# A hybrid decoder step: the split weights begin at eight byte offsets

## The chip, the cores and the metric

The kernel runs on one core of one Trainium2 chip. The metric is the device time of one execution in microseconds (us). The kernel before took 1399.37 us, the median of three runs (1398.88 to 1400.08).

## What is computed

One inference step of one decoder layer for 256 prompt tokens and 8 sample tokens, 264 columns in all, with a model width of 2048, in float32. What matters here is that it is mostly products of activations with large weight matrices:

```python
def _layer(x, mem_k, mem_v, k_buf, v_buf, ssd_conv_past, ssd_h0, ffn_past, w):
    proj = rms_norm(x, w['g_mix']) @ w['w_in']                 # 2048 x 6688
    q, k, v, z, xbc, dt_raw = jnp.split(proj, IN_SPLITS, axis=-1)
    ...
    x = x + jnp.concatenate([attn, ssd], axis=-1) @ w['w_out']  # 3072 x 2048
    x = x + cross_attend(x, mem_k, mem_v, w['g_cross'], w['w_cq'], w['cq_norm_g'], w['w_co'])
    f, new_ffn = conv_ffn(x, ffn_past, w['g_ffn'], w['w_up'], w['ffn_conv_w'], w['ffn_conv_b'],
                          w['w_down'])                          # 2048 x 11264, 5632 x 2048
    return x + f, (new_k, new_v, new_conv, new_h, new_ffn)
```

Between the products lie a sliding-window attention, a Mamba-2 scan, a cross-attention into 256 memory tokens and two short convolutions.

## The kernel before, in words

Activations are kept with features on the partitions and the 264 tokens along the free dimension: a tile of eight blocks holds 8 x 264 float32 values in each partition, so one block begins 1056 bytes behind the last. Each float32 operand of a large product is split into a high part, rounded to the type float32r, and a low part, which is the difference. Three products of the parts, each a float32r matmul, stand for one float32 product: high x high, high x low, low x high. That is `mm3` (lines 99 to 102): for each 128 x 128 block of weights, line 100 multiplies the high weights with the high activations, line 101 the high weights with the low activations, line 102 the low weights with the high activations. The weights are the stationary operand, so every matmul has its own weight load; only in `v_pair`, for the matrix w_cv, the memory tokens are stationary and the weights move.

`weights` (line 72) brings a weight unit of 2048 float32 values per partition in two parts of 1024 (NPART). For each part it issues one DMA from SyncE's queue into a buffer `wraw` (line 79), casts it to the high tile `whi` on ScalarE (line 85) and subtracts on VectorE to the low tile `wlo` (line 86). Each of the three tags has four buffers of 4096 bytes per partition (WBUFS is 4, line 67), used in turn; a buffer is written again when TensorE has done with the part that lay in it. The pool of these tiles is allocated ahead of the pools of the activations, and the sizes are multiples of 32 bytes.

`proj` (line 104) loops over units, over the parts of a unit, over two output blocks m and over the four k of a part, and calls `mm3`: a part is 2 x 4 x 3 = 24 matmuls, and the slice of weights that one matmul loads begins at k x 1024 + m x 512 bytes within the part. The first part of a unit goes with the activation blocks k 0 to 3 of a tile of eight, the second with k 4 to 7. For an output accumulated in a PSUM bank, `evac` takes it out on VectorE.

The opening of the kernel works on eight parts that arrive in blocks together with the activations; `w_piece` (line 171) allocates their high and low tiles from the same buffers and cuts them into two k of 512 columns. Everything after it goes through `weights`. An `up` block of the feed-forward stage multiplies two units of w_up with the activations X2 (x2h, x2l), a `down` block one unit of w_down with hh and hl.

Three other places are touched by the prediction: line 1359 writes the tile u from its element 2 (`u[:, 2:]`), line 1404 adds a result to the aligned slices of the residual, and lines 686 and 708 are the sample attention's matmuls with the cached keys kcT (rows of 129 elements) and values vc (rows of 128).

The order of most work is left to a planner that keeps the program's order per engine, with priorities for the weights; the opening is in an order written out by hand.

Of the kernel before, what the change touches and what calls it, by code (L numbers as in the profile page):

```python
# [8 lines left out]
F32R = mybir.dt.float32r  # L9
# [38 lines left out]
def hybrid_decoder_step_kernel(ctx: ExitStack, tc: tile.TileContext, I, O):  # L48
# [4 lines left out]
    wpool = ctx.enter_context(tc.tile_pool(name="wpool", bufs=2))  # L53
# [6 lines left out]
    def psum(tag):  # L60
        return ps.tile([128, 512], F32, tag=tag, name=tag, bufs=banks[tag])
# [4 lines left out]

    NPART, WBUFS = 1024, 4

    def raw_part(n=NPART):
        return wpool.tile([128, n], F32, tag="wraw", name="wraw", bufs=4)  # L70

    def weights(src, n=2048, into=None):

        out = []
        with tc.high_priority():
            for o in range(0, n, NPART):
                w = min(NPART, n - o)
                x = raw_part(w)
                nc.sync.dma_start(out=x, in_=src[:, o:o + w])
                if into:  # L80
                    hi, lo = into
                else:
                    hi = wpool.tile([128, w], F32R, tag="whi", name="whi", bufs=WBUFS)
                    lo = wpool.tile([128, w], F32R, tag="wlo", name="wlo", bufs=WBUFS)
                S.copy(out=hi, in_=x)  # L85
                V.tensor_tensor(out=lo, in0=x, in1=hi.bitcast(F32), op=ALU.subtract)  # L86
                out.append((hi, lo))
        return out
# [15 lines left out]
    def proj(units, acts, evac, n=T, nb=2, tag="mm"):  # L104

        outs = [psum(t) for t in (tag if isinstance(tag, list) else [tag] * nb)]
        for ui, (src, act) in enumerate(zip(units, acts)):
            parts = src if isinstance(src, list) else weights(src)
            for pi, (wh, wl) in enumerate(parts):
                wh = wh.rearrange("p (k c) -> p k c", c=128 * nb)  # L110
                wl = wl.rearrange("p (k c) -> p k c", c=128 * nb)
                nk = wh.shape[1]
                for m in range(nb):
                    for k in range(nk):
                        kk = pi * nk + k
                        ah, al = act(8 * ui + kk) if callable(act) else (act[0][:, kk, :n], act[1][:, kk, :n])
                        last = mm3(outs[m][:, :n], wh[:, k, m * 128:(m + 1) * 128], wl[:, k, m * 128:(m + 1) * 128],
                            ah, al,
                            ui == 0 and kk == 0, ui == len(units) - 1 and kk == nk * len(parts) - 1)
                if ui == 0:  # L120
                    marks["part"] = last
        for m in range(nb):
            with tc.high_priority():
                evac(m, outs[m][:, :n])
# [44 lines left out]
    pre = {}  # L169

    def w_piece(k, n):
        if k % 2 == 0:
            pre[k // 2] = [wpool.tile([128, NPART], F32R, tag=t, name=t, bufs=WBUFS).rearrange("p (k c) -> p k c", c=512)
                           for t in ("whi", "wlo")]
        return blocks[k // 4][:, k % 4:k % 4 + n, T:], *(w[:, k % 2:k % 2 + n, :] for w in pre[k // 2])

    def w_split(k, n, half=False):
        raw, hi, lo = w_piece(k, n)
        if half:
            V.tensor_copy(out=hi[:, :, 0:256], in_=raw[:, :, 0:256])  # L180
            S.copy(out=hi[:, :, 256:512], in_=raw[:, :, 256:512])
        else:
            S.copy(out=hi, in_=raw)
        return lambda: V.tensor_tensor(out=lo, in0=raw, in1=hi.bitcast(F32), op=ALU.subtract)
# [9 lines left out]
    with tc.manual_schedule(engines={mybir.EngineType.SP, mybir.EngineType.PE, mybir.EngineType.Activation, mybir.EngineType.DVE}):  # L194
# [21 lines left out]
        for k in range(6):  # L216
            x_hi(k)
            lo = w_split(k, 1, k < 2)
            x_lo(k)
            lo()  # L220
        for k in range(6, KB, 2):
            x_hi(k)
            x_hi(k + 1)
            lo = w_split(k, 2)
# [200 lines left out]
    p = psum("y")  # L425
# [40 lines left out]
    p = psum("x")  # L466
# [5 lines left out]
    p = psum("x")  # L472
# [301 lines left out]
    for c in range(2):  # L774
        p = psum("x")
# [4 lines left out]
    for w, XT in enumerate((BT, CT)):  # L780
        p = psum("x")
# [71 lines left out]
    p = psum("x")  # L853
# [349 lines left out]
    def v_pair(i):  # L1203
        pv = [psum("mm") for _ in range(2)]
        for u in range(2):
            parts = [w.rearrange("p (k c) -> p k c", c=256) for hl in weights(I["w_cv"][2 * i + u]) for w in hl]
            nk = parts[0].shape[1]
            for k in range(8):
                wh, wl = parts[2 * (k // nk)], parts[2 * (k // nk) + 1]
                mhi, mlo = mem_hl(8 * u + k)  # L1210
                for c in range(2):
                    cs = slice(c * 128, c * 128 + 128)
                    mm3(pv[c][:, 0:256], mhi[:, cs], mlo[:, cs], wh[:, k % nk, :], wl[:, k % nk, :],
                        u + k == 0, u == 1 and k == 7)
        for c in range(2):
            S.activation(out=vx[:, c, 256 * i:256 * i + 256], in_=pv[c][:, 0:256], func=AF.Copy, scale=rmc[:, 0, c:c + 1])
# [15 lines left out]
    p = psum("y")  # L1232
# [45 lines left out]
    for pi, (wh, wl) in enumerate(weights(I["w_co"][0])):  # L1278
        wh, wl = (w.rearrange("p (k c) -> p k c", c=512) for w in (wh, wl))
        for k in range(2):  # L1280
            h = 2 * pi + k
            for m in range(4):
                ms = slice(m * 128, m * 128 + 128)
                mm3(outs[m][:, :T], wh[:, k, ms], wl[:, k, ms], OH[:, h, :], OL[:, h, :], h == 0, h == 3)
# [4 lines left out]
    for u in range(1, 4):  # L1289
        with tc.issue_after(heads[0].ins), tc.issue_after(heads[1].ins):  # L1290
            proj([I["w_co"][u]], [(OH, OL)], lambda m, pm, u=u: x2_ev(4 * u + m, pm), nb=4,
                 tag=[cyc[(4 * (u - 1) + m) % 5] for m in range(4)])
# [264 lines left out]
def build(shapes):  # L1557

    import concourse.bacc as bacc

    nc = bacc.Bacc("TRN2", target_bir_lowering=False, num_devices=1)
    ins = {n: nc.dram_tensor(f"in_{n}_dram", s, dt, kind="ExternalInput").ap() for n, (s, dt) in shapes.items()}
    outs = {n: nc.dram_tensor(f"out_{n}_dram", s, F32, kind="ExternalOutput").ap() for n, s in _OUTS}
    with tile.TileContext(nc, schedule_with_timeline_sim=True) as tc:
        hybrid_decoder_step_kernel(tc, ins, outs)
    return nc
# [10 lines left out]
```

## Time and profile before

| | |
|---|---|
| median of three runs | 1399.37 us (1398.88 to 1400.08) |
| span of the profiled execution, first to last instruction | 1397.1 us |
| the median less that span | 2.3 us |
| TensorE matmul, busy | 1392.5 us, 11535 matmuls |
| weight loads (PEld), busy | 1367.8 us, 11535 loads |
| VectorE, busy | 1052.1 us (75%) |
| ScalarE, busy | 769.3 us (55%) |
| GpSimd, busy | 95.4 us (7%) |
| moved by DMA | 298.33 MB, mean 214 GB/s |

In the rows of the profile, PE is TensorE's matmul, PEld its weight load, DVE VectorE, ACT ScalarE, POOL GpSimd and SP SyncE. L85 is line 85 of the kernel. A row of a group names the output and input tiles (without buffer numbers), the shapes, the count, the busy time in us and the mean ns of one, and the idle time of the engine just before them with what ended most of it. Matmuls overlap, and their ends are modelled, so the busy time of PE is no measure of how well it is used; the starts of the instructions are.

### The profile page before, as it was taken

To read this page: it belongs to the slowest core of one execution; us is meant where nothing else is said; L and a number is where in the kernel's file an instruction comes from. 1 tells how busy PE (TensorE), PEld (TensorE's weight loads), DVE (VectorE), ACT (ScalarE), POOL (GpSimd) and SP (SyncE) were. 2 spreads that over 40 slices of the span, in tenths; PEclk is the share of its full clock that TensorE was granted. 3 is DMA by queue.
4 is the path that set the end of the run, shared out by engine and by line. 5 is a ranking of instruction groups with operands and counts; after the bars stand their busy time and mean duration, and the time that the engine had idled before them with its cause. 6 is when DMAs were issued, how large, how long until landed. Compare 5 with 4: busy or idle time off the path is not lost.

```text
span 1397.1 us, 29012 instructions
## 1 busy us (share of the span) xinstructions
PE 1392.5 (100%) x11535; PEld 1367.8 (98%) x11535; DVE 1052.1 (75%) x1874; ACT 769.3 (55%) x1255; POOL 95.4 (7%) x286
## 2 busy tenths in 40 slices
PE   9999999999999999999999999999999999999999
PEld 9999999999999999899999999999999999999998
DVE  7879799999987774578777775777577757765654
ACT  7667756556545554566565544554455445543532
POOL 0000011121000000002010000000000000000000
PEclk9999999999999999999999999999999999999999
DMA  7954467777777567565576765676567656655664
GB/s 299 323 162 135 139 217 245 233 239 253 235 221 240 182 237 263 209 251 191 186 255 213 255 208 187 211 254 211 185 211 239 197 184 197 196 180 183 191 185 138
DMA packets 89479, 298.33 MB, mean 214 GB/s; under 512 B 12032, under 2 KB 17152, under 8 KB 88832
## 3 DMA queue, kind: packets, MB, share of 16 engines
q1 hardware_dynamic: 83840, 277.61, 60.5%
q0 software_dynamic: 5504, 18.88, 4.1%
q8 instruction: 90, 1.47, 0.4%
q14 instruction: 45, 0.37, 0.1%
HBM read 280.77 MB, written 16.23 MB: 213 GB/s over the span
## 4 chain that ended last, share of the span: by engine, by line
PE 100%; DVE 0%; issue 0%
PE mm L100 21%; PE mm L101 21%; PE mm L102 21%; PE t L100 10%; PE t L102 10%; PE t L101 10%; PE t L240 1%; PE y L825 1%; PE t L278 1%; PE y L841 0%; PE s L240 0%; PE mm L240 0%; PE x L278 0%; PE t L559 0%; PE x L1137 0%; PE s L1184 0%
## 5 line engine op out<-in xcount | busy, mean ns | idle before, releaser
L85 ACT CAST whi<-wraw 128x1024 fp32r<-128x1024 f32 x440 | 459.9, 1048 | 530.6 <-PE mm L101 278.3
L86 DVE TENSOR_TENSOR wlo<-wraw,whi 128x1024 fp32r<-128x1024 f32 x440 | 541.8, 1233 | 221.1 <-ACT whi L85 217.3
L100 PE MATMUL mm<-x2h,whi 128*128 128x264 f32 x704 | 199.8, 284 | 0.0
L100 PE MATMUL t<-x2h,whi 128*128 128x264 f32 x704 | 199.8, 284 | 0.0
L102 PE MATMUL t<-x2h,wlo 128*128 128x264 f32 x704 | 199.7, 284 | 0.0
L101 PE MATMUL mm<-x2l,whi 128*128 128x264 f32 x704 | 199.6, 284 | 0.0
L101 PE MATMUL t<-x2l,whi 128*128 128x264 f32 x704 | 199.5, 283 | 0.0
L102 PE MATMUL mm<-x2h,wlo 128*128 128x264 f32 x704 | 199.3, 283 | 0.0
L101 PE MATMUL mm<-hl,whi 128*128 128x264 f32 x704 | 198.7, 283 | 0.0
L102 PE MATMUL mm<-hh,wlo 128*128 128x264 f32 x704 | 198.2, 283 | 0.0
L100 PE MATMUL mm<-hh,whi 128*128 128x264 f32 x704 | 197.2, 284 | 0.0
L100 PE MATMUL mm<-xh,whi 128*128 128x264 f32 x576 | 164.7, 287 | 0.0
L101 PE MATMUL mm<-xl,whi 128*128 128x264 f32 x576 | 164.5, 287 | 0.0
L102 PE MATMUL mm<-xh,wlo 128*128 128x264 f32 x576 | 162.8, 287 | 0.0
L101 PEld LDWEIGHTS mm<-x2l,whi 128*128 128x128 f32 x704 | 132.6, 188 | 0.0
L100 PEld LDWEIGHTS t<-x2h,whi 128*128 128x128 f32 x704 | 132.5, 188 | 0.0
L101 PEld LDWEIGHTS t<-x2l,whi 128*128 128x128 f32 x704 | 132.5, 188 | 0.0
L101 PEld LDWEIGHTS mm<-hl,whi 128*128 128x128 f32 x704 | 132.4, 188 | 0.0
L100 PEld LDWEIGHTS mm<-x2h,whi 128*128 128x128 f32 x704 | 132.4, 188 | 0.0
L102 PEld LDWEIGHTS t<-x2h,wlo 128*128 128x128 f32 x704 | 132.2, 188 | 0.0
L102 PEld LDWEIGHTS mm<-x2h,wlo 128*128 128x128 f32 x704 | 132.1, 188 | 0.0
L102 PEld LDWEIGHTS mm<-hh,wlo 128*128 128x128 f32 x704 | 132.0, 188 | 0.0
(506 smaller groups left out, 2950.7 us busy)
## 6 DMA issues: line engine op xcount, KB each, us to landing
wraw<-in_w_up_dram SPq DMA_DIRECT2D x176, 512.0 KB, 4.4
wraw<-in_w_in_dram SPq DMA_DIRECT2D x96, 512.0 KB, 4.7
wraw<-in_w_dn_dram SPq DMA_DIRECT2D x88, 512.0 KB, 4.3
wraw<-in_w_out_dram SPq DMA_DIRECT2D x48, 512.0 KB, 4.4
h<-in_h_dram POOLq DMA_DIRECT2D x32, 256.0 KB, 4.6
hn<-in_h_dram SPq DMA_DIRECT2D x16, 512.0 KB, 4.8
out_state_s_dram<-hn POOLq DMA_DIRECT2D x16, 512.0 KB, 3.5
e<-dram_la SPq DMA_DIRECT2D x16, 256.0 KB, 5.5
```

Source lines behind the costliest of these rows:

```text
L85: S.copy(out=hi, in_=x)
L86: V.tensor_tensor(out=lo, in0=x, in1=hi.bitcast(F32), op=ALU.subtract)
L100: PE.matmul(out, wh, xh, start=start, stop=False)
L101: PE.matmul(out, wh, xl, start=False, stop=False)
L102: return PE.matmul(out, wl, xh, start=False, stop=stop)
L240: PE.matmul(first[c][:, :T], pre[k // 2][i][:, k % 2, c * 128:(c + 1) * 128], A[k // 8][x][:, k % 8, :], start=k + i + x == 0, stop=k == K ...
L278: return PE.transpose(out, in_, cst[0:k, C_ID:C_ID + k])
L825: PE.matmul(y[o:o + 64, (h // 2) * 128:(h // 2) * 128 + 128], xdt[:, h, :], es[h // 4][:, h % 4, :], start=True, stop=True)
```

## The change

The buffers of `whi` and `wlo` become 24 float32 elements (96 bytes) longer, and a part no longer begins at the start of its buffer: the high part begins at the element that a list of eight gives for the part's number modulo 8, the low part at another entry, which shifts by one every eight parts. In bytes the entries are 0, 16, 32, 48, 64, 80, 8 and 4. The eight parts of the opening keep offset 0 in the longer buffers. The four buffers of a tag lie 4192 bytes apart instead of 4096, and the tiles allocated behind them move by 768 bytes. `wraw`, the number and kind of the instructions and their order are left as they are.

```diff
     NPART, WBUFS = 1024, 4
 
+    WSLACK, WSTART = 24, (0, 4, 8, 12, 16, 20, 2, 1)
+    part_no = [0]
+
+    def offsets():
+        n = part_no[0]
+        part_no[0] += 1
+        return WSTART[n % 8], WSTART[(n + n // 8) % 8]
+
...
-                    hi = wpool.tile([128, w], F32R, tag="whi", name="whi", bufs=WBUFS)
-                    lo = wpool.tile([128, w], F32R, tag="wlo", name="wlo", bufs=WBUFS)
+                    hi, lo = (wpool.tile([128, NPART + WSLACK], F32R, tag=t, name=t, bufs=WBUFS)[:, a:a + w]
+                              for t, a in zip(("whi", "wlo"), offsets()))
...
-            pre[k // 2] = [wpool.tile([128, NPART], F32R, tag=t, name=t, bufs=WBUFS).rearrange("p (k c) -> p k c", c=512)
+            pre[k // 2] = [wpool.tile([128, NPART + WSLACK], F32R, tag=t, name=t, bufs=WBUFS)[:, 0:NPART].rearrange("p (k c) -> p k c", c=512)
```

## The prediction

> **What bounds the kernel now.** I read the page from the top: busy times, the chain of work that ended last, then the groups.
>
> ```profile
> span 1397.1 us, 29012 instructions
> PE 1392.5 (100%) x11535; PEld 1367.8 (98%) x11535; DVE 1052.1 (75%) x1874; ACT 769.3 (55%) x1255; POOL 95.4 (7%) x286
> ...
> PE 100%; DVE 0%; issue 0%
> ...
> L85 ACT CAST whi<-wraw 128x1024 fp32r<-128x1024 f32 x440 | 459.9, 1048 | 530.6 <-PE mm L101 278.3
> L86 DVE TENSOR_TENSOR wlo<-wraw,whi 128x1024 fp32r<-128x1024 f32 x440 | 541.8, 1233 | 221.1 <-ACT whi L85 217.3
> L100 PE MATMUL mm<-x2h,whi 128*128 128x264 f32 x704 | 199.8, 284 | 0.0
> ```
>
> TensorE is on the chain for all of the span, so whatever happens to one matmul or one weight load is paid 10,000 times over, and whatever happens to ScalarE or VectorE is not paid until it makes TensorE late. The two instructions that write the tiles of this change have that room: the 440 casts on ScalarE have 530.6 us of idle time just before them, 278.3 of it spent on TensorE to let go of a buffer; the 440 subtractions on VectorE have 221.1 us, nearly all of it spent on the cast. They are made ahead of need and held up by TensorE, not the reverse.
>
> The 284 ns in the L100 row is how long one matmul is in flight, not what it costs, because matmuls overlap. Their cost is the time between starts. The windows view of 100 us each, in the middle of the feed-forward stage, gives it:
>
> ```profile
> 900.00:1000.00 100.00, 100.00 (x828) 100.00 (x828) 68.98 (x115) 50.60 (x78) 6.57 (x27) 1.00 0.68 217
> 1000.00:1100.00 100.00, 100.00 (x828) 100.00 (x828) 74.86 (x134) 57.80 (x100) 8.86 (x40) 1.00 0.66 217
> ```
>
> The columns are the stretch, its length, and the busy time and count of PE, PEld, DVE, ACT and POOL, then the granted clock (1.00), the DMA share and GB/s. 828 matmuls in 100 us are 100,000 / 828 = 120.8 ns from start to start, with as many weight loads, in both windows and with TensorE at its full clock. The change can only move the time by moving these 120.8 ns, or by breaking the cover above.
>
> **Does a start address matter at all?** Nothing in the page says so, so I looked at matmul starts one by one. The timeline of TensorE in one unit and a half of the up-projection, first matmul (L100) of the steps that matter:
>
> ```profile
> 742.52 0.28 PE L100 MATMUL mm<-x2h,whi 128*128 128x264 f32 x1
> ...
> 743.61 0.28 PE L100 MATMUL mm<-x2h,whi 128*128 128x264 f32 x1
> 743.97 0.28 PE L100 MATMUL mm<-x2h,whi 128*128 128x264 f32 x1
> ...
> 745.41 0.28 PE L100 MATMUL mm<-x2h,whi 128*128 128x264 f32 x1
> ...
> 746.50 0.29 PE L100 MATMUL mm<-x2h,whi 128*128 128x264 f32 x1
> 746.87 0.28 PE L100 MATMUL mm<-x2h,whi 128*128 128x264 f32 x1
> ...
> 748.34 0.28 PE L100 MATMUL mm<-x2h,whi 128*128 128x264 f32 x1
> ...
> 751.23 0.28 PE L100 MATMUL mm<-x2h,whi 128*128 128x264 f32 x1
> ...
> 754.15 0.28 PE L100 MATMUL t<-x2h,whi 128*128 128x264 f32 x1
> ```
>
> A part is 24 matmuls (two output blocks, four k, three products each), so the rows at 742.52, 745.41, 748.34, 751.23 and 754.15 are the starts of four parts and of the next unit. The parts took 2.89, 2.93, 2.89 and 2.92 us. The first part of a unit meets k 0 to 3 of its activations and the second k 4 to 7, and the short and the long one alternate though the weights sit in another of the four buffers each time. Inside a part, three matmuls of one k take 0.36 us (743.61 to 743.97) or 0.37 us (746.50 to 746.87). What differs between those steps is where the moving operand begins: by the code, weights are at the same place modulo 512 bytes in every step (buffers of 4096 bytes, slices of 512), while activations advance by 264 x 4 = 1056 bytes per k, which is 32 past a multiple of 512. So the interval does depend on position, by some 1% either way between parts of a unit. That is the only lever this change has, and it is a small one.
>
> How far a single matmul swings shows in the spread of durations (min/median/max) that the view of the tile whi gives:
>
> ```profile
> L101 PEld LDWEIGHTS mm<-x2l,whi x704: 187/188/192, 625.8 to 1311.8; 128*128 128x128 f32 x176
> L101 PE MATMUL mm<-x2l,whi x704: 278/284/288, 625.9 to 1311.9; 128*128 128x264 f32 x176
> ```
>
> Over 704 loads the load itself takes 187 to 192 ns; the matmul beside it 278 to 288, so 6 ns below the median at best and 4 above it at worst.
>
> **The change, part by part.** *The longer buffers* (4192 bytes for 4096) add no instruction. They put the four buffers of a tag at +0, +96, +192 and +288 bytes relative to the old grid, and everything allocated behind them 8 x 96 = 768 bytes on. *The offsets* add 0, 16, 32, 48, 64, 80, 8 or 4 bytes (elements 0, 4, 8, 12, 16, 20, 2, 1 of the list), a fixed one for the high tile and a rotating one for the low tile. All 440 casts, subtractions and loads stay, in number, size and order; no wait, DMA or queue is touched.
>
> *Multiples of 32 bytes* (three of eight parts for each tile). Step by step the moving operand already walks through all sixteen positions in steps of 32 bytes against the weights' fixed place modulo 512. Moving the weights by such a multiple permutes combinations that occur today. Mean over a unit before: (2.89 + 2.93 + 2.89 + 2.92) / 4 = 2.91 us per part; mean after, over the same set in another order: the same. Ends: every part becomes like the short ones, 2.91 - 2.89 = 0.02 us, times 440 = -9 us; or like the long ones, +0.02 us, +9 us. I take 0, since the mix stays uniform.
>
> *Odd multiples of 16* (three of eight) and *8 and 4 bytes* (two of eight). No load of before begins at such a place, so the price of it for a stationary operand isn't in the trace. The nearest rows are a moving operand, in the sample attention:
>
> ```profile
> 174.00 1.09 PE L686 MATMUL s<-kcT,zz 128*32 128x129 f32 x32
> ...
> 187.93 1.08 PE L708 MATMUL s<-vc,zz 128*32 128x128 f32 x32
> ```
>
> By the code kcT has rows of 129 elements, so its sixteen slices begin at every multiple of 4 bytes in turn; vc has rows of 128 and all its slices begin on 512. The 32 matmuls take 1.09 and 1.08 us, and the odd one has a column more in each. A start inside a few bytes costs the moving operand nothing that shows. For a load the bounds are: 6 ns below (the whole swing to the fastest matmul, 284 to 278) and 4 ns above (284 to 288). Of the 440 parts, the eight of w_cv are the moving operand, so (440 - 8) x 24 = 10,368 loads count; two in eight of them, 2,592, begin at 4 or 8 bytes. Ends for those: 2,592 x 4 ns = +10.4 us and 2,592 x -6 ns = -15.6 us. The value I take is 0, because the kcT row is the only one with such starts.
>
> [...]
>
> *The writers.* ScalarE now writes the high tile, VectorE reads it and writes the low one, at such starts. The row for a write:
>
> ```profile
> L1404 DVE TENSOR_TENSOR res<-mm,res 128x264 f32<-128x264 f32 x96 | 40.9, 428 | 55.6 <-PE mm L102 55.6
> L1359 DVE TENSOR_TENSOR u<-mm,r 128x264 f32<-128x264 f32 x44 | 18.8, 429 | 8.2 <-PE mm L102 8.1
> ```
>
> Line 1404 writes an aligned slice, line 1359 writes u from element 2, which is 8 bytes in; 428 and 429 ns. So nothing for VectorE. For ScalarE I have no such row; a tenth of its 1048 ns less or more per cast are my bounds; less only lengthens its idle time, and more, 440 x 0.105 = 46 us, would lie in the 530.6 us of it. Where the cover is thin is the stretch in which VectorE is nearly full:
>
> ```profile
> 200.00:300.00 100.00, 100.00 (x840) 97.31 (x840) 98.21 (x189) 56.96 (x99) 18.79 (x24) 1.00 0.74 240
> 300.00:400.00 100.00, 100.00 (x825) 96.05 (x824) 97.39 (x185) 55.59 (x96) 13.88 (x17) 1.00 0.74 239
> ```
>
> The subtractions of line 86 alone in the same stretches:
>
> ```profile
> 200.00:300.00 100.00, 36.80 (x30) 1.00 0.74 240
> 300.00:400.00 100.00, 39.55 (x32) 1.00 0.74 239
> ```
>
> VectorE is busy 98% of these 200 us, 76.35 of them with 62 subtractions. If these grew by 5%, 3.8 us would come to light, and 5% less would bring at most as much. I take 0, by line 1359, and keep 4 us either way.
>
> *The sum*: 0 + 0 + 0 + 0. The profiled execution has a span of 1397.1 us; the median of the runs, 1399.37, is 2.3 us more, which lies around the span and isn't touched. **I predict 1399.4 us, no change.** From here on "no change" is within 0.2%, 2.8 us, about what a measurement of this kernel can tell.
>
> **Rivals.** *Slower: loads that begin inside a 16-byte line are late (0.24).* The place is the load of a high or low slice in the two parts in eight with 4 or 8 bytes. With 2,592 of them, the point from which it decides is 2.8 us / 2,592 = 1.1 ns each; half of the upper bound, 2 ns, gives 1399.4 + 5.2 = 1404.6 us; all of it 1409.8. For it: TensorE has no slack, and it would be paid in full. Against it: the kcT row, and loads of 188 ns that begin every 120.8 ns overlap the matmuls ahead of them, so a nanosecond more may be hidden. [...]
>
> *Faster: the fixed place of the weights is what makes some steps slow (0.24).* Each unit now repeats the same slow steps 88 times. If reads of weights and activations get in each other's way, a start on an odd multiple of 16 could step out of it. Up to all parts like the short ones: 1399.4 - 9 = 1390.4 us; if only the three in eight with 16-byte steps gain, 3/8 of 9 = 3.4: 1396.0. For it: the alternating 2.89 and 2.93, at a full clock and with no wait. Against it: the steps already pass through all sixteen positions and none of them gives a part under 2.89.
>
> [...]
>
> *Slower: the writers (0.04)*, the +4 us of VectorE's full stretch: 1403.4 us. *Faster: the 768 bytes by which all later tiles move (0.02)* change which activation positions meet: by the same 0.02 us per part, at most -9 us, 1390.4.
>
> **How the numbers follow.** No change 0.46; slower 0.24 + 0.04 = 0.28; faster 0.24 + 0.02 = 0.26. Range: downwards into the faster rival, past its 16-byte case (1396.0), to 1394; upwards past the 2 ns case (1404.6) to 1407. What is left out is the last third of either rival, about 0.08 on each side. The likeliest case's own range is 1396.6 to 1402.2.
>
> **What would show it.** Right: 827 to 829 matmuls in windows of 100 us of the feed-forward stage; L85 and L86 within 10 ns of 1048 and 1233; the short and the long part no longer alternating by unit, but with eight kinds of part around 2.91 us. Wrong towards slower: loads or matmuls of the 4- and 8-byte parts longer than their neighbours, and fewer than 826 a window. Wrong towards faster: more than 830, with the parts of odd 16-byte starts the short ones. The prediction falls altogether if a start that is no multiple of 32 has a price or a gain of more than a nanosecond per load.

## The result: 5 us slower, and the profile after

| | before | after |
|---|---|---|
| median of five runs | 1399.32 us (1398.88 to 1400.08) | 1404.40 us (1403.66 to 1404.67) |
| span of the profiled execution | 1397.1 us | 1402.2 us |
| ratio of the times, 95% interval | | 1.0035 (1.0021 to 1.0049) |

The change makes the kernel slower by 0.35%, more than the 0.2% that counts as no change. The page of the changed kernel, at the lines that answer to those of before (the cast is line 93 now, the subtraction line 94, the three matmuls lines 108 to 110):

```profile
span 1402.2 us, 29012 instructions
...
PE 1397.3 (100%) x11535; PEld 1371.9 (98%) x11535; DVE 1051.8 (75%) x1874; ACT 768.9 (55%) x1255; POOL 95.0 (7%) x286
...
L93 ACT CAST whi<-wraw 128x1024 fp32r<-128x1024 f32 x440 | 459.5, 1047 | 535.7 <-PE mm L109 298.9
L94 DVE TENSOR_TENSOR wlo<-wraw,whi 128x1024 fp32r<-128x1024 f32 x440 | 541.6, 1232 | 224.9 <-ACT whi L93 221.0
```

The count of instructions is the same, the cast takes 1047 ns (1048 before) and the subtraction 1232 (1233), and ScalarE waits for TensorE rather longer than before (298.9 us in place of 278.3). So the writers cost nothing, and the 5.1 us of span are TensorE's own. The windows view, with the columns as in the prediction:

```profile
900.00:1000.00 100.00, 100.00 (x825) 100.00 (x824) 69.48 (x118) 50.47 (x79) 6.79 (x29) 1.00 0.65 218
1000.00:1100.00 100.00, 100.00 (x825) 100.00 (x824) 73.60 (x129) 57.88 (x99) 8.21 (x38) 1.00 0.63 212
```

825 matmuls in 100 us in place of 828, or 121.2 ns for 120.8 from start to start, at the same clock. The loss is spread over the kernel. The view of whi gives the first and last start of the x2h matmuls, before (L100) and after (L108, and L109 for x2l):

```profile
L100 PE MATMUL mm<-x2h,whi x704: 280/283/290, 625.8 to 1311.8; 128*128 128x264 f32 x176
```
```profile
L108 PE MATMUL mm<-x2h,whi x704: 278/284/292, 627.6 to 1316.7; 128*128 128x264 f32 x176
L109 PE MATMUL mm<-x2l,whi x704: 278/284/293, 627.7 to 1316.8; 128*128 128x264 f32 x176
```

1.8 us have been lost by the first of them, at 627.6 in place of 625.8, and 689.1 - 686.0 = 3.1 us more by the last. The parts of the unit that the prediction looked at (starts of four parts and of the next unit, from the timeline of TensorE):

```profile
744.87 0.28 PE L108 MATMUL mm<-x2h,whi 128*128 128x264 f32 x1
...
747.78 0.28 PE L108 MATMUL mm<-x2h,whi 128*128 128x264 f32 x1
...
750.71 0.28 PE L108 MATMUL mm<-x2h,whi 128*128 128x264 f32 x1
...
753.63 0.28 PE L108 MATMUL mm<-x2h,whi 128*128 128x264 f32 x1
...
756.56 0.28 PE L108 MATMUL t<-x2h,whi 128*128 128x264 f32 x1
```

The parts take 2.91, 2.93, 2.92 and 2.93 us, where they took 2.89, 2.93, 2.89 and 2.92: the short first halves are gone. Over the 212 parts of the feed-forward stage that both timelines show in full, by their starts, the first half of a unit went from 120.49 ns a matmul to 121.48, with a spread of 0.48 among parts; the second half went from 121.77 to 121.76, with a spread of 0.51 where there had been next to none (under 0.1). Most combinations of a high and a low start have an interval of their own: the changed kernel has 64 in this stage, with medians from 120.6 to 122.8 ns, and 184 of 263 parts lie within 0.1 ns of the median of theirs. The kernel before had a good one, 120.5 ns, in every first half.

### The profile page after: what moved, and what is told of

Read it like the earlier page. It is cut to its first block, busy times and chain, and to the rows that moved or that the text cites. A ratio compares the mean times of both kernels' runs of the same rounds, so it can differ in the third digit from the quotient of the medians.

```text
span 1402.2 us, 29012 instructions
## 1 busy us (share of the span) xinstructions
PE 1397.3 (100%) x11535; PEld 1371.9 (98%) x11535; DVE 1051.8 (75%) x1874; ACT 768.9 (55%) x1255; POOL 95.0 (7%) x286
## 4 chain that ended last, share of the span: by engine, by line
PE 99%; DMA 0%; SPq 0%; ACT 0%; DVE 0%; issue 0%
PE mm L108 21%; PE mm L110 21%; PE mm L109 21%; PE t L108 10%; PE t L110 10%; PE t L109 10%; PE t L248 1%; PE y L833 1%; PE t L286 1%; PE y L849 0%; DMA open<-in_open_dram 0%; PE x L286 0%; PE t L567 0%; PE mm L248 0%; PE s L248 0%; PE x L1145 0%
## 5 line engine op out<-in xcount | busy, mean ns | idle before, releaser
L93 ACT CAST whi<-wraw 128x1024 fp32r<-128x1024 f32 x440 | 459.5, 1047 | 535.7 <-PE mm L109 298.9
L94 DVE TENSOR_TENSOR wlo<-wraw,whi 128x1024 fp32r<-128x1024 f32 x440 | 541.6, 1232 | 224.9 <-ACT whi L93 221.0
L108 PE MATMUL t<-x2h,whi 128*128 128x264 f32 x704 | 200.3, 285 | 0.0
L108 PE MATMUL mm<-x2h,whi 128*128 128x264 f32 x704 | 200.0, 284 | 0.0
L109 PE MATMUL mm<-x2l,whi 128*128 128x264 f32 x704 | 200.0, 284 | 0.0
L109 PE MATMUL t<-x2l,whi 128*128 128x264 f32 x704 | 199.9, 284 | 0.0
L109 PE MATMUL mm<-hl,whi 128*128 128x264 f32 x704 | 199.2, 284 | 0.0
L108 PE MATMUL mm<-hh,whi 128*128 128x264 f32 x704 | 197.5, 284 | 0.0
L108 PE MATMUL mm<-xh,whi 128*128 128x264 f32 x576 | 165.0, 288 | 0.0
L109 PE MATMUL mm<-xl,whi 128*128 128x264 f32 x576 | 164.5, 287 | 0.0
L108 PEld LDWEIGHTS t<-x2h,whi 128*128 128x128 f32 x704 | 132.6, 188 | 0.0
L109 PEld LDWEIGHTS mm<-x2l,whi 128*128 128x128 f32 x704 | 132.6, 188 | 0.0
L109 PEld LDWEIGHTS t<-x2l,whi 128*128 128x128 f32 x704 | 132.6, 188 | 0.0
L109 PEld LDWEIGHTS mm<-hl,whi 128*128 128x128 f32 x704 | 132.5, 188 | 0.0
L108 PEld LDWEIGHTS mm<-x2h,whi 128*128 128x128 f32 x704 | 132.5, 188 | 0.0
```

Source lines behind the costliest of these rows:

```text
L108: PE.matmul(out, wh, xh, start=start, stop=False)
L109: PE.matmul(out, wh, xl, start=False, stop=False)
```

## The experiments

Theory A, formed on this: the interval depends on the place of the weights against the activations, that is, on the difference of their start addresses modulo 256 bytes, and before's place in the first halves is a good one that the change gives up. Rival B is the prediction's: a load that begins 4 or 8 bytes past a multiple of 16 is late, by 2 ns for 5.1 us over 2,592 loads. The 16-byte line in its name is an assumption of mine; no run shows one.

**The longer buffers alone.**

```diff
-    WSLACK, WSTART = 24, (0, 4, 8, 12, 16, 20, 2, 1)
+    WSLACK, WSTART = 24, (0, 0, 0, 0, 0, 0, 0, 0)
```

> The buffers are 96 bytes longer as in the change, but every part begins at the start of its buffer, so all starts are multiples of 32 bytes. Theory A (the kernel before has a placement of weights against activations that suits the first half of each unit, 120.5 ns from matmul to matmul, and nearly any other placement costs about 121.6): still slower than before, by 3 to 6 us; the first-half parts of the feed-forward stage rise from 120.5 to 121 to 122 ns, the second-half parts stay near 121.8. Rival B (a load that begins 4 or 8 bytes into a 16-byte line costs about 2 ns): back to the time of before, within 1 us.

Measured: 1400.63 us, ratio 1.0011 (1.0002 to 1.0020), so 1.4 us slower. Less than theory A expected, more than rival B. Buffers on steps of 96 bytes have only four places, each met again and again: first halves at 120.91 ns, up by 0.4, second halves at 121.24 and 121.94.

**All starts on multiples of 16 bytes.**

```diff
-    WSLACK, WSTART = 24, (0, 4, 8, 12, 16, 20, 2, 1)
+    WSLACK, WSTART = 24, (0, 4, 8, 12, 16, 20, 8, 4)
```

> The change, with the entries of 8 and 4 bytes replaced by 32 and 16 bytes, so that no load begins inside a 16-byte line. Theory A: as slow as the change, 4 to 6 us over before. Rival B: all of the change's 5.1 us goes, within 1 us of before.

Measured: 1404.54 us, ratio 1.0038 (1.0025 to 1.0051). With every start on a multiple of 16 bytes the kernel is as slow as the change. Rival B falls.

**Every part 4 bytes in.**

```diff
-    WSLACK, WSTART = 24, (0, 4, 8, 12, 16, 20, 2, 1)
+    WSLACK, WSTART = 24, (1, 1, 1, 1, 1, 1, 1, 1)
```

> The longer buffers of the first experiment, with every high and low part 4 bytes in. All 10,368 loads of the weights then begin inside a line. Theory A: the time of the first experiment of this group, within 1.5 us, and the same interval for each of its parts within 0.3 ns. Rival B: 10,368 loads at 2 ns, some 20 us over the first experiment.

Measured: 1403.02 us, ratio 1.0028 (1.0017 to 1.0040), 2.4 us over the longer buffers alone, not 20; and more than theory A allowed. Its four places show why it is no price per load: 4 bytes more moved them from 120.90 to 120.94, from 120.92 to 121.60, from 121.24 to 120.97 and from 121.94 to 122.08 ns. One of four became faster. On average a load pays 2.4 us / 10,368 = 0.23 ns, where rival B had 2 ns. Four bytes act as a change of place like any other.

One row of the windows view of each of the three, in the order above, with 828 before and 825 after the change:

```profile
1000.00:1100.00 100.00, 100.00 (x827) 100.00 (x826) 74.36 (x134) 58.11 (x101) 8.86 (x40) 1.00 0.66 214
```
```profile
1000.00:1100.00 100.00, 100.00 (x824) 100.00 (x823) 73.74 (x130) 57.63 (x99) 8.18 (x38) 1.00 0.64 212
```
```profile
1000.00:1100.00 100.00, 100.00 (x826) 100.00 (x825) 74.18 (x132) 57.61 (x100) 8.78 (x40) 1.00 0.65 212
```

So no run here shows the rival's price for weight loads that begin off a multiple of 16 bytes: the second of these runs, which has no such start, is no faster than the change (1404.54 and 1404.40 us), and the third, in which every load has one, is 2.4 us slower than the first, not 20.

**The activations 128 bytes on, weights as before.**

```diff
     wpool = ctx.enter_context(tc.tile_pool(name="wpool", bufs=2))
+    gap = ctx.enter_context(tc.tile_pool(name="gap", bufs=1)).tile([128, 32], F32, name="gap")
+    P.memset(gap, 0.0)
     apool = ctx.enter_context(tc.tile_pool(name="apool", bufs=1))
```

> The kernel before, with 128 unused bytes between the weights' buffers and the activations, so that all activations move by 128 bytes against the weights. Theory A, with the relative place modulo 256 bytes as what counts: the first half of a unit (k 0 to 3) now meets the places that the second half had and the other way round, so the first-half parts take 121.8 and the second-half parts 120.5 ns, and the time stays within 1 us of before. If position counts modulo more than 256, or history more than place: both halves near 121.6, and 4 to 5 us over before. Rival B expects no change in either.

The starts of four parts and of the next unit:

```profile
743.00 0.28 PE L102 MATMUL mm<-x2h,whi 128*128 128x264 f32 x1
...
745.92 0.28 PE L102 MATMUL mm<-x2h,whi 128*128 128x264 f32 x1
...
748.81 0.28 PE L102 MATMUL mm<-x2h,whi 128*128 128x264 f32 x1
...
751.73 0.28 PE L102 MATMUL mm<-x2h,whi 128*128 128x264 f32 x1
...
754.62 0.28 PE L102 MATMUL t<-x2h,whi 128*128 128x264 f32 x1
```

2.92, 2.89, 2.92, 2.89: the halves have changed roles. Over the parts of the up-projection the first half takes 121.8 ns and the second 120.5, the old pair of numbers exchanged; in the down-projections the exchange is less clean (121.6 and 121.0, where before had 120.6 and 121.6). The time is 1400.38 us, ratio 1.0007 (0.9998 to 1.0015), 1.15 us over before where theory A had allowed 1. The place counts, and the exchange fits places counted modulo 256.

**Weights and activations 64 bytes on together; then the activations alone.** Two kernels with a gap of 16 elements, one ahead of the pool of the weights, one behind it.

> The kernel before with 64 unused bytes ahead of the weights' buffers, so that weights and activations move by 64 bytes together and the place of one against the other stays. Theory A: no change, within 1 us of before, 120.5 and 121.8 ns for the two halves. Rival D (the addresses themselves count, not the difference): the halves leave these values, towards 121.6 each.

> The kernel before with 64 unused bytes between the weights' buffers and the activations: the weights' place against the activations moves by 64 bytes, with all starts still multiples of 32. Theory A: a place not met before, near the mean of all places, about 121.6 in both halves, 3 to 7 us over before. My prediction's step (a shift by a multiple of 32 only permutes what occurs anyway): within 1 us of before.

Together: 1399.51 us, ratio 1.0000 (0.9992 to 1.0009), halves at 120.49 and 121.77 as before. The activations alone: 1403.62 us, ratio 1.0030 (1.0018 to 1.0041), halves at 121.57 and 121.49. Rival D falls: for this shift of 64 bytes only the difference of the addresses matters. And a shift by a plain multiple of 32 bytes, with whole units and nothing else changed, costs 4.2 us, which is most of what the change costs. A row of each, together first:

```profile
1000.00:1100.00 100.00, 100.00 (x828) 100.00 (x827) 74.89 (x134) 57.80 (x100) 8.86 (x40) 1.00 0.67 216
```
```profile
1000.00:1100.00 100.00, 100.00 (x826) 100.00 (x825) 73.64 (x130) 57.90 (x99) 8.18 (x38) 1.00 0.66 212
```

**Both halves at the good place; both at the other.** Four buffers become two tags of two, used in turn; those of the second half begin 128 bytes on. With a second gap ahead of the activations both halves have the place of before's first half, without it that of the second.

```diff
+    def hi_lo():
+        n = part_no[0] % 2
+        part_no[0] += 1
+        if n and not gap:
+            gap.append(wodd.tile([128, 32], F32, tag="gap", name="gap", bufs=1))
...
+        return [(wodd if n else wpool).tile([128, NPART], F32R, tag=t, name=t, bufs=WBUFS) for t in ("whi", "wlo")]
```

> The kernel before with its four buffers split into two tags of two, and the buffers of the second half of each unit 128 bytes on, so that the weights of both halves begin where their first activation block begins, modulo 256 bytes. Nothing else changes. Theory A (the interval is set by the place of the weights against the activations modulo 256): both halves at 120.5 ns, so 216 parts x 24 x 1.3 ns = 6.7 us under before, some 1392.5 us: faster than both kernels. Rival C (any departure from buffers at one regular step costs, whatever the place): 1 to 5 us over before, the halves near 121.6.

> The same two tags, but without the second gap ahead of the activations, so that both halves meet the place that the second half has in the kernel before (128 bytes off). Theory A: both halves at 121.8 ns, 6.7 us over before, some 1406 us. Rival C: as in the run with both halves at the fast place.

Good place: 1399.85 us, ratio 1.0005 (0.9996 to 1.0014). Other place: 1407.76 us, ratio 1.0059 (1.0046 to 1.0071). A row of each:

```profile
1000.00:1100.00 100.00, 100.00 (x827) 100.00 (x826) 74.78 (x134) 57.70 (x100) 8.86 (x40) 1.00 0.67 216
```
```profile
1000.00:1100.00 100.00, 100.00 (x821) 100.00 (x821) 71.43 (x123) 55.56 (x93) 7.61 (x37) 1.00 0.64 212
```

The second is slower as theory A had it, if by 8.4 us rather than 6.7; the first gains nothing, and there the theory failed. With the good place in both halves every part takes 121.2 ns, not 120.5; with the other, 122.08, not 121.8. So the place of before's first half gives 120.5 ns behind a part of the other kind and not behind one of its own: what went before a matmul counts as well as its own place. Rival C, that any irregular buffers cost, does not explain 1399.85 beside 1407.76 either.

**One place for a whole unit pair.** This kernel and the one of the last experiment leave out part of the computation; each was executed once, with the profile.

```diff
-            proj([w_up[2 * i], w_up[2 * i + 1]], X2, ev, tag="t" if i % 2 else "mm")
+            def same(q, j=i % 8):
+                return X2[q // 8][0][:, j, :], X2[q // 8][1][:, j, :]
+
+            proj([w_up[2 * i], w_up[2 * i + 1]], [same, same], ev, tag="t" if i % 2 else "mm")
```

> The kernel before, with its weights and buffers as they are, but in the up-projection all sixteen k of block i multiply the same activation block, number i modulo 8 of its tile, in place of k's own; so this part of the computation is changed, with the same instructions in the same order. Within one i the place of the weights against the activations is then constant, at 32 x (i modulo 8) bytes modulo 256. Theory A (each place has its interval): eight levels of interval, each constant within its i, between some 117 and 125 ns, their mean near 121. Rival E (what costs is the change of place from one matmul to the next, or the history of the places): one level for all eight, below 120 ns.

The starts of eight pairs of units with i from 8 to 15, each of 96 matmuls, and of what comes next:

```profile
719.11 0.28 PE L100 MATMUL mm<-x2h,whi 128*128 128x264 f32 x1
...
730.76 0.29 PE L100 MATMUL t<-x2h,whi 128*128 128x264 f32 x1
...
742.49 0.28 PE L100 MATMUL mm<-x2h,whi 128*128 128x264 f32 x1
...
754.10 0.28 PE L100 MATMUL t<-x2h,whi 128*128 128x264 f32 x1
...
765.78 0.29 PE L100 MATMUL mm<-x2h,whi 128*128 128x264 f32 x1
...
777.62 0.29 PE L100 MATMUL t<-x2h,whi 128*128 128x264 f32 x1
...
789.31 0.28 PE L100 MATMUL mm<-x2h,whi 128*128 128x264 f32 x1
...
800.85 0.29 PE L100 MATMUL t<-x2h,whi 128*128 128x264 f32 x1
...
812.38 0.28 PE L100 MATMUL mm<-hh,whi 128*128 128x264 f32 x1
```

Differences over 96: 121.4, 122.2, 120.9, 121.7, 123.3, 121.8, 120.2 and 120.1 ns at places 0, 32, 64 and so on to 224 bytes. These are levels, and every i with the same place returns to its level within 0.3 ns, but for two: i = 0, which ran at 120.15 at place 0 where the later ones ran at 121.3, and i = 1, which other matmuls interrupt. At a constant place the starts settle into short cycles, such as 118, 123, 125 ns at 32 bytes and 122, 118 at 224. The levels are theory A's, in a narrower band (120.1 to 123.3) than it had. Rival E falls: a constant place doesn't bring one level below 120, it fixes the level. One place with two levels is history again.

**A constant place in the real computation.** This one does all of the work, with the weights laid out on the activations' step of 1056 bytes:

```diff
+    def part_tile(t):
+        return wpool.tile([128, 4 * 264], F32R, tag=t, name=t, bufs=WBUFS)
+
+    def rows(t):
+        return t.rearrange("p (s c) -> p s c", c=264)[:, :, SHIFT:SHIFT + 256]
+
+    def block(w, k, m, nb):
+        e = (k * nb + m) * 128
+        return w[:, e // 256, e % 256:e % 256 + 128]
...
+                    hi, lo = rows(part_tile("whi")), rows(part_tile("wlo"))
+                x = x.rearrange("p (s c) -> p s c", c=256)
```

SHIFT is 8 elements in the first kernel and 0 in the second.

> The same computation as before, all of it, with another layout of the weights: a part is four rows of 256 columns that lie 1056 bytes apart, as the activation blocks do, in buffers of 4224 bytes, and begins 32 bytes into its buffer. For 9,944 of the 10,560 matmuls that load these weights the activations then begin 224 bytes behind the weights, modulo 256, all the time. To make room two small tags lose a buffer and one tile shares a buffer with others. Theory F (the interval is set by the place, and by the places just before it, and a constant place of 224 bytes settles at 120.0 ns, as it did with one block per i): 1.1 ns under before's 121.1 over 10,400 matmuls, 11 us faster, 1387 to 1390 us, and 832 to 833 matmuls in 100 us. Rival G (the strided writes of the weights or the changed buffers cost what is gained): no faster than before.

> The same kernel with the parts at the start of their buffers, 32 bytes earlier, so that the constant place is 0 bytes. Theory F: 121.3 ns, as with one block per i at that place; some 2 us slower than before, 1400 to 1403 us, or, if it settles in the other state that one i showed there, 120.15 ns and 1389 us. Rival G: the same time as with the constant place of 224 bytes.

224 bytes: 1396.57 us, ratio 0.9980 (0.9971 to 0.9989). 0 bytes: 1405.25 us, ratio 1.0043 (1.0029 to 1.0057). A row of each, and of the first also the starts of two pairs of units:

```profile
1000.00:1100.00 100.00, 100.00 (x832) 100.00 (x832) 74.73 (x135) 58.26 (x101) 8.90 (x40) 1.00 0.65 219
```
```profile
1000.00:1100.00 100.00, 100.00 (x826) 100.00 (x825) 72.92 (x127) 57.56 (x98) 8.13 (x37) 1.00 0.65 212
```
```profile
730.57 0.28 PE L110 MATMUL t<-x2h,whi 128*128 128x264 f32 x1
...
742.20 0.28 PE L110 MATMUL mm<-x2h,whi 128*128 128x264 f32 x1
...
904.62 0.29 PE L110 MATMUL mm<-x2h,whi 128*128 128x264 f32 x1
...
916.18 0.29 PE L110 MATMUL t<-x2h,whi 128*128 128x264 f32 x1
```

The first beats both kernels, by 2.7 us against before, and reaches the 832 matmuls of theory F in these windows; but it is a quarter of the 11 us expected. Of two pairs of units with the same placing, one takes 11.63 us (121.1 ns) and a later one 11.56 (120.4): the level changed behind the first stretch of down-projections and stayed. The second is slower than theory F had it, by 2 us. Rival G falls as the whole account, since both kernels write the weights in the same strides and differ by 8.7 us, and the cast of the first takes 1046 ns, no longer than before.

**One of the two readers on one address.**

```diff
+                        if flat:
+                            w2 = [w[:, 0:1].broadcast_to([128, 128]) for w in w2]
...
+            def one(q):
+                return [x[:, q % 8, 0:1].broadcast_to([128, T]) for x in X2[q // 8]]
+
+            proj([w_up[2 * i], w_up[2 * i + 1]], [one, one] if i % 3 == 1 else X2, ev, tag="t" if i % 2 else "mm", flat=i % 3 == 2)
```

> The kernel before, with part of the up-projection changed by i modulo 3, with the same instructions in the same order: at 0 as before; at 1 the moving operand of each matmul is one column of its activation block, read 264 times (a step of 0); at 2 each load reads one column of its weights 128 times. One of the two readers then stays on one address. Theory H (a load and the matmul that runs beside it read SBUF at the same time, and where their addresses meet one of them waits; that is what the place sets): at 1 and at 2 the intervals no longer vary with k and fall from 121.1 to 112 to 117 ns; at 0 they keep 121.1. Rival I (the variation arises inside TensorE, not from reading): all three keep some 121 ns and a pattern by k.

The starts of i = 21 (as before), 22 (the moving operand reads one element), 23 (each load reads one element), and of what comes next:

```profile
910.77 0.28 PE L100 MATMUL t<-x2h,whi 128*128 128x264 f32 x1
...
922.40 0.27 PE L100 MATMUL mm<-x2h,whi 128*128 128x264 f32 x1
...
933.20 0.28 PE L100 MATMUL t<-x2h,whi 128*128 128x264 f32 x1
...
944.76 0.28 PE L100 MATMUL mm<-hh,whi 128*128 128x264 f32 x1
```

11.63, 10.80 and 11.56 us for 96 matmuls: 121.1, 112.5 and 120.4 ns. With the moving operand on one element all starts are 111 to 113 ns apart, whatever k; with the loads on one element they still go from 117 to 124 by k. From i = 3 on, the other i of each kind lie within 0.1 ns of these. Theory H holds for the one and not for the other. The 8.6 ns a matmul go when the moving operand stays on one element, and nearly all of them are still there when the load does: a walk of the load is not needed for them. The whole run agrees: 1,440 matmuls with a still moving operand at 8.6 ns and 1,344 with a still load at 0.7 make 13.3 us, and it took 1386.14 us, 13.1 less than before's 1399.22.

## Why the prediction was right or wrong, point by point

- *TensorE is on the chain throughout, and the time moves only with the 120.8 ns.* Right: 121.2 after, with everything else as it was.
- *Position matters, by some 1% between parts of a unit.* Right, and the exchange of the halves (120.5 and 121.8 ns) with the activations 128 bytes on shows it.
- *Multiples of 32 bytes: 0, since the mix stays uniform.* Wrong, and this is the step that failed. The activations alone on by 64 bytes cost 4.2 us, at 121.5 ns in both halves against 120.5 and 121.8. The sixteen positions were all there before, but a mean over positions is not kept when they are met in another order or with another pair of high and low tile: the interval also depends on what ran just before (at the place of before's first half, 120.5 ns behind a part of the other kind and 121.2 behind one of its own). The mean of before is that of one lucky sequence. Of some 75 distinct pairs of places for the high and low tiles that before, the change and the first four experiments met, before's first half has the lowest mean (120.5), and the mean of all is 121.6. Before's two halves together have 121.1. The ends I gave, 9 us either way, did hold the 5.1 us. With these means known, the forecast would have been +0.5 ns x 10,400 = 5 us, the way from a good draw to the mean; the trace of before alone did not have them.
- *Odd multiples of 16, and 8 and 4 bytes: 0.* No price per load: without the 4- and 8-byte starts the change is as slow (1404.54 and 1404.40 us). They act as places like any others. In the changed kernel the parts with a tile 4 or 8 bytes in are no slower than the rest (121.6 ns a matmul in both).
- *The writers: 0.* Right, 1047 and 1232 ns.
- *The 768 bytes, 0.02.* They are three times 256, so by themselves they leave every place, counted modulo 256, as it was; together with the longer buffers they cost 1.4 us.
- *Rival: late loads at 4 and 8 bytes, 1404.6 us.* The number is that of the measurement and the mechanism is not; a match of a total proves nothing about its cause. No run shows the 2 ns a load in that sum, nor a line of 16 bytes: what the runs showed is 0.23 ns a load on average with every load 4 bytes in (1403.02 us for 1400.63).
- *Rival: the fixed place makes some steps slow, faster when spread.* The other way round: the fixed place made some parts fast. A fixed place chosen on purpose does gain, 2.7 us.
- *The forecast of no change*, at 0.46, did not come true; the measured time lies within the range, on the side to which I gave 0.28. That it lies within is luck: the upper end was taken from the rival's case of 2 ns for loads at 4 and 8 bytes, and the runs show another cause.
- *The signs.* The 825 matmuls a window are under the 826 named as the sign of a slower kernel, but the other half of that sign, slow parts at 4 and 8 bytes, did not show. No start that is no multiple of 32 had a price or a gain above a nanosecond per load on average (0.23 ns with every load 4 bytes in). What falls is the argument on multiples of 32, which no sign was set for.

What is left open: why the level at one place depends on what went before. A state that is carried from one matmul to the next would do it, but no run looked inside. Nor is it shown whether the 8.6 ns are a cost of the moving reads alone or of their meeting the loads: a load on one address may still read. And a moving operand on one element also has one value in all its columns; no run separates the walk from the change of values.

## What to carry to other kernels

Where an engine is full and its instructions are short, look at the time from start to start, position by position in the loop, before calling an address harmless: here it was parts that kept alternating at 2.89 and 2.93 us, at a clock of 1.00, that showed the place at work. Don't argue that a reshuffle keeps a mean: the layout at hand may be a good draw, and any other is then likely to be worse. Of the ten other placings run here, seven were slower by more than noise, two the same and one faster. And to find what a layout costs, put one operand on a single address and see what the interval falls to (here from 121.1 to 112.5 ns).

## What the runs showed of the hardware that was not expected

A float32r matmul of 264 columns with its own weight load took 112.5 ns from start to start when its moving operand read one element, and 121.1 ns when it read its 264 in a row: 8.6 ns, 7% of each matmul. If all 10,368 lose as much, that is some 89 us of this kernel, by my estimate; the run that shows it leaves out work, so it is no saving that a right kernel has shown. With each load on one element instead, it took 120.4 ns. The place of the weights against the activations, modulo 256 bytes, moved the walking one between 120.1 and 123.3 ns at constant places. Moving both by 64 bytes cost nothing (1399.51 us, ratio 1.0000) and moving the activations alone 4.2 us (1403.62 us), so here the interval depends on the places of the two together; whether they meet at the reads, no run shows.
